# Hybrid pooling and gated-DeltaNet block on one core: the row-scale broadcast and the first pool product written as split fp32r matmuls

## The chip, the cores and the metric

One Trainium2 chip, one of its cores. The kernel is one program, launched once. The metric is the device time of that launch in microseconds. The engines are named as the profile names them: PE is TensorE (PEld its weight loads), DVE is VectorE, ACT is ScalarE, POOL is GpSimd, SP is SyncE. A "q" behind an engine's name means its queue, for instance SPq for the transfers that SP issues.

## What is computed

One decoder block on x of 2048 rows by 1024 columns, all in float32, cut here to what the change touches:

```
n    = x * rsqrt(mean(x*x, per row) + eps) * norm_w          # row scale r = rsqrt(...)
proj = n @ w_in                                               # 1024 -> 3080 columns
pool_u, pool_z, q, k, v, z, b, a = split(proj)
# pool branch: 4 groups of 128 channels, trailing windows 2, 4, 8, 16
mix  = trailing_mean(pool_u, window of the group) - pool_u
pool = (mix @ pool_w[group]) * pool_scale * silu(pool_z)
# DeltaNet branch: 4 heads of 128, causal conv of width 4 on q, k, v, chunked delta rule
h    = x + [pool ; deltanet] @ w_out
out  = rms_norm(h, final_norm_w)
```

## The kernel before

**Layout of the work.** The 2048 rows are worked in two blocks (`b` 0 and 1) of 1024 rows, each in two halves (`hf` 0 and 1) of 512. Channels lie on the 128 partitions and rows along the free axis, so that a projection tile is a 128x512 PSUM tile. Products that must be accurate are made of split operands: a float32 value is written as a high part in fp32r and a low part, the remainder, in fp32r, and three fp32r matmuls (high by high, high by low, low by high) are added in PSUM. `project` (L727) does this with eight contraction steps of three matmuls each (L733, L734, L735). Other products are single float32 matmuls, which the profile shows as two PE instructions each.

**The row scale.** The projections multiply x times norm_w; the row scale r is applied to the result. For each half, `square_x` (L531) sums the squares of the eight column tiles on ACT, DVE and POOL. `row_scale` (L543) sums them over the partitions with four one-column float32 matmuls into `pss`, computes r by an integer guess and three Newton steps on 128x4 tiles (DVE, L501 to L508), and writes four 128x128 diagonal matrices `dg`, ident times r (L557, a tile with the tag `sacc`). `broadcast` (L559) multiplies a matrix of ones by these 512 columns in float32 (`psr`, L561), which puts r of each row on all partitions, and ACT copies the result to `rb` (L563). Each evacuation of a projection tile out of PSUM multiplies by `rb` (L742, L758, L771), and so does the gate's (L574). No PSUM bank of a half's projections comes free before its `rb` is there.

**The pool branch.** In each half, `pool_mix` (L767) makes the mix of a group. For groups 1 to 3 the pool weights have been multiplied into the projection weights (`mix_weights`, L691), and `pool_out` (L794) only scales. For group 0, `pool_out` multiplies mix by `pw[:, 0]` in one float32 matmul of 512 columns (`pm`, L798), and DVE scales the result out of PSUM (L800).

**What sets the order.** Each step is entered with a slot number (`at(slot, function)`), and slots give the program order. `Planner.run` then makes the order of each engine: a list schedule over all instructions with a cost for each (L123, where a float32 matmul of 512 columns is put at 860 ns and an fp32r one at 226 ns), with latest times computed backwards, in which PE takes whole groups of matmuls and may take a group up to 24 places ahead if it can start sooner (L282 to L292), and the other engines take the most urgent ready instruction unless that would delay a more urgent one. Each engine executes the order so made, strictly in turn. `L_ROW0`, `L_RB` and the like are hand-set distances in slots. Tiles come from rings by tag: `acc` has three buffers, `sacc`, `ps_s` and `sqj` two, `tmp` and `X` one; a new tile of a tag waits until the tile that had its buffer is read for the last time.

**The opening.** `begin` (L457) loads norm_w and fills `ones`, `warm_up` (L461) runs 11 float32 matmuls on it, `load_constants` (L466) issues nine small loads on SP, `prepare_constants` (L486) makes the fp32r constants.

Of the kernel before, what the change touches and what calls it, by code (L numbers as in the profile page):

```python
# [43 lines left out]
PAIRED = 2  # L44
# [353 lines left out]
def hymba_kernel(  # L398
# [44 lines left out]
    ones = ct([P, P], F32, "ones")  # L443
    ones_r = ct([P, P], F32R, "ones_r")
    wba = ct([P, KT, 8], F32, "wba")
# [4 lines left out]
    pw = ct([P, GROUPS, P], F32, "pw")  # L450
# [5 lines left out]

    def begin():  # L457
        nc.scalar.dma_start(nw, norm_w)
        nc.vector.memset(ones, 1.0)

    def warm_up():  # L461
        ps = plan.tile(pd, [P, HALF], F32, "pd", "warm", 2, True)
        for i in range(WARM):
            nc.tensor.matmul(ps[:, 0:P], ones, ones, start=True, stop=True)

    def load_constants():  # L466
        plan.opening = len(plan.traced)
        tri = st([P, 2, P], F32, "X")
        for dst, src in (
# [6 lines left out]
            (pw, pool_w),  # L476
# [7 lines left out]
        return tri  # L484

    def prepare_constants(tri):  # L486
# [56 lines left out]
    def row_scale(env):  # L543
        ps = plan.tile(pd, [P, HALF], F32, "pd", "pss", 2, True)
        for j in range(NCH):
            nc.tensor.matmul(
                ps[:, j : j + 1], env["ss"][:, j * P : (j + 1) * P], ones[:, 0:1], start=True, stop=True
            )
# [6 lines left out]
        env["dg"] = dg = st([P, NCH, P], F32, "sacc", 2)  # L555
        for j in range(NCH):
            nc.vector.tensor_scalar(out=dg[:, j], in0=ident, scalar1=r[:, j : j + 1], scalar2=None, op0=ALU.mult)  # L557

    def broadcast(env):  # L559
        ps = plan.tile(pd, [P, HALF], F32, "pd", "psr", 2, True)  # L560
        nc.tensor.matmul(ps, ones, env["dg"].rearrange("p a b -> p (a b)"), start=True, stop=True)  # L561
        env["rb"] = rb = st([P, HALF], F32, "rb", 3)
        nc.scalar.copy(rb, ps)  # L563
# [127 lines left out]
    def mix_weights(gi, m, part):  # L691
        ks = slice(part * NCH, (part + 1) * NCH)
        ps = plan.tile(pd, [P, NCH, P], F32, "pd", "pw", 2, True)
        for j in range(NCH):
            nc.tensor.matmul(ps[:, j], m["wT"][:, part * NCH + j], pw[:, gi], start=True, stop=True)
# [71 lines left out]
    def pool_mix(u, b, gi, hf, rb):  # L767
# [24 lines left out]
        )  # L792

    def pool_out(u, b, gi, hf, res, mixed_w):  # L794
        pm = u["mix"]
        if not mixed_w:
            pm = plan.tile(pp, [P, HALF], F32, "pp", "pm", 3, True)
            nc.tensor.matmul(pm, pw[:, gi], u["mix"], start=True, stop=True)  # L798
# [299 lines left out]
    lead = 1  # L1098
    for i, gi in enumerate(range(lead, GROUPS)):
# [4 lines left out]
    tri = []  # L1104
    at(-90, begin)
    at(-89, warm_up)
    at(-45, lambda: tri.append(load_constants()))
    at(-1, lambda: prepare_constants(tri[0]))
    for b in range(NB):
# [5 lines left out]
        for gi, res in pools[:lead]:  # L1115
# [4 lines left out]
        for gi, res in pools[lead:]:  # L1120
# [39 lines left out]
        for (kind, et, idx, res), hf in order:  # L1160
            if et not in weights:
                weights[et] = {"mixed": kind == "pu" and idx >= lead}
# [383 lines left out]
```

## Time and profile before

| what | value |
|---|---|
| time, median of 3 runs | 945.32 us (944.15 to 946.16) |
| time of the profiled execution | 946.3 us |
| its span, first to last instruction | 944.6 us |
| granted TensorE clock, mean | 0.995 of full |
| PE busy | 917.4 us, 97% |
| DVE busy | 659.9 us, 70% |
| ACT busy | 467.3 us, 49% |
| POOL busy | 146.9 us, 16% |

The profile records one execution. Its span leaves out 1.7 us of the 946.3 us around the first and the last instruction. Matmuls overlap in the records: a matmul's own duration is longer than the distance to the next one's start, and that distance is what it costs in a stream. "Idle before" an instruction is time in which its engine ran nothing, and the name behind the arrow is the instruction whose end released it.

### The profile page before, as it was taken

The page shows a single profiled execution, that of the slowest core. Times are in us where ns is not written, and L with a number is a line of the kernel's source. Part 1 is how long each engine was busy: PE and PEld are TensorE (multiplying, and loading weights), DVE is VectorE, ACT ScalarE, POOL GpSimd, SP SyncE. Part 2 cuts the span into 40 slices and gives each one's busy share as a digit, 9 for nine tenths or more (in the row PEclk, how much of TensorE's full clock was granted, in tenths as well). Part 3 has the DMA queues.
Part 4 walks back from the last instruction along what each step waited for, and adds up shares of the span by engine and source line. Part 5 has one row for each costly group of instructions (what it writes and reads, how often), then busy time and mean ns, then how long its engine had stood idle before and what let it go on. Part 6 is the DMA issues. An engine that isn't in the chain of part 4 may idle for free.

```text
span 944.6 us, 15009 instructions
## 1 busy us (share of the span) xinstructions
PE 917.4 (97%) x5226; PEld 741.2 (78%) x5226; DVE 659.9 (70%) x1963; ACT 467.3 (49%) x1209; POOL 146.9 (16%) x195
## 2 busy tenths in 40 slices
PE   8999999999999999999999999999999999999995
PEld 6667888888888877768888787887887788788884
DVE  7587976867768455865886774875854578987665
ACT  7338654464464245534945544545533435444441
POOL 3206210110100012302610010011001000011110
PEclk9999999999999999999999999999999999999998
DMA  8424564344433554434345343334247487466644
GB/s 290 107 57 95 140 168 106 67 100 93 94 89 87 156 146 141 103 74 89 97 104 115 73 89 86 73 84 112 56 119 252 120 230 227 140 168 168 165 104 122
DMA packets 82268, 115.84 MB, mean 123 GB/s; under 512 B 31888, under 2 KB 49552, under 8 KB 82192
## 3 DMA queue, kind: packets, MB, share of 16 engines
q0 software_dynamic: 17280, 56.89, 27.6%
q1 hardware_dynamic: 64480, 57.46, 19.6%
q8 instruction: 41, 0.67, 0.3%
q10 hardware_dynamic: 432, 0.53, 0.2%
q14 instruction: 35, 0.29, 0.1%
HBM read 92.83 MB, written 22.02 MB: 122 GB/s over the span
## 4 chain that ended last, share of the span: by engine, by line
PE 70%; DVE 9%; issue 8%; DMA 6%; ACT 3%; POOL 1%; SPq 1%; DVEq 0%; ACTq 0%; POOLq 0%
PE ps L733 14%; PE ps L735 13%; PE ps L734 13%; PE psA L1399 2%; PE psA L1400 2%; PE psA L1401 2%; PE tp L825 2%; PE ch L1012 2%; PE ch L990 1%; DMA wl<-in_w_in_dram 1%; PE ch L1006 1%; PE ob L1000 1%; PE ob L1016 1%; PE psC L1401 1%; PE psC L1400 1%
## 5 line engine op out<-in xcount | busy, mean ns | idle before, releaser
L733 PE MATMUL ps<-nh,wh 128*128 128x512 f32 x768 | 326.1, 425 | 0.9 <-ACT nh L526 0.4
L735 PE MATMUL ps<-nh,wl 128*128 128x512 f32 x768 | 302.4, 394 | 2.4 <-DMA wl<-in_w_in_dram 2.4
L734 PE MATMUL ps<-nl,wh 128*128 128x512 f32 x768 | 301.4, 392 | 2.2 <-DVE nl L527 2.2
L735 PEld LDWEIGHTS ps<-nh,wl 128*128 128x128 f32 x768 | 144.5, 188 | 35.6 <-DMA wl<-in_w_in_dram 4.1
L734 PEld LDWEIGHTS ps<-nl,wh 128*128 128x128 f32 x768 | 145.7, 190 | 27.1 <-DVE nl L527 5.0
L733 PEld LDWEIGHTS ps<-nh,wh 128*128 128x128 f32 x768 | 145.5, 189 | 26.2 <-issue 1.6
L747 DVE SCALAR_TENSOR_TENSOR acc<-u,cw,acc 128x512 f32<-128x512 f32 x144 | 109.5, 760 | 19.0 <-ACT acc L745 16.7
L716 POOL DMA_DIRECT2D wh<-in_w_in_dram x40 | 22.3, 557 | 342.5 <-PE ps L735 330.3
L742 DVE TENSOR_TENSOR u<-ps,rb 128x512 f32<-128x512 f32 x48 | 33.1, 689 | 51.4 <-PE ps L735 51.2
L724 ACT ACTIVATE wl<-wh 128x1024 fp32r<-128x1024 f32 x40 | 42.5, 1061 | 47.9 <-DMA wh<-in_w_in_dram 34.9
L725 POOL DMA_DIRECT2D wl<-in_w_in_dram x40 | 34.8, 871 | 186.6 <-ACT wl L724 146.9
L905 DVE TENSOR_TENSOR tmp<-Ai,X 128x60 f32<-128x60 f32 (+24 forms) x248 | 53.4, 215 | 7.4 <-DMA Ai<-blocks 1.6
L911 DVE TENSOR_TENSOR X<-X,tmp 128x60 f32<-128x60 f32 (+24 forms) x248 | 53.6, 216 | 6.2
L745 ACT ACTIVATE acc<-u,cw 128x512 f32<-128x512 f32 x48 | 34.9, 727 | 45.6 <-DVE u L742 43.3
L1019 ACT ACTIVATE sqj<-v 128x128 f32<-128x128 f32 x64 | 19.7, 308 | 65.8 <-DVE v L1017 59.6
L1008 ACT ACTIVATE nv<-ch,sm 128x128 f32<-128x128 f32 x64 | 23.5, 368 | 32.1 <-PE ch L1006 32.1
L1407 POOL DMA_DIRECT2D dec<-in_x_dram x23 | 19.7, 854 | 122.8 <-ACT dec L1406 69.7
L1013 DVE SCALAR_TENSOR_TENSOR state<-state,ex,ch 128x128 f32<-128x128 f32 x64 | 22.0, 344 | 20.7 <-PE ch L1012 19.9
L832 ACT ACTIVATE sqj<-tp 128x128 f32<-128x128 f32 x128 | 33.7, 278 | 4.5 <-PE tp L825 4.3
L1002 ACT ACTIVATE o<-ob,ex 128x128 f32<-128x128 f32 x64 | 23.6, 369 | 18.8 <-PE ob L1000 17.8
L1012 PEld LDWEIGHTS ch<-nv,kdec 128*128 128x128 f32 x128 | 19.7, 189 | 13.5 <-ACT nv L1008 12.9
L1006 PEld LDWEIGHTS ch<-rho,Tt 128*128 128x128 f32 x128 | 22.3, 189 | 8.2 <-DVE rho L992 4.6
(299 smaller groups left out, 1768.6 us busy)
## 6 DMA issues: line engine op xcount, KB each, us to landing
wh<-in_w_in_dram POOLq DMA_DIRECT2D x40, 512.0 KB, 3.9
wl<-in_w_in_dram POOLq DMA_DIRECT2D x40, 512.0 KB, 5.5
y_dram<-yt SPq DMA_DIRECT2D x32, 256.0 KB, 2.9
out_dram<-dec SPq DMA_DIRECT2D x14, 512.0 KB, 3.7
dec<-in_x_dram POOLq DMA_DIRECT2D x23, 256.0 KB, 4.1
Ai<-blocks SPq DMA_DIRECT2D x32, 128.0 KB, 2.6
yr<-y_dram SPq DMA_DIRECT2D x8, 512.0 KB, 4.8
dec<-in_xT_dram SPq DMA_DIRECT2D x7, 512.0 KB, 6.6
```

The costliest lines, as they stand in the source:

```text
L724: nc.scalar.activation(w["lo"], w["hi"].bitcast(F32), AF.Copy, scale=-1.0)
L725: nc.gpsimd.dma_start(w["lo"], w_in[et], accum_op=ALU.add)
L733: nc.tensor.matmul(ps, w["hi"][:, k], nh[:, k], start=(k == 0), stop=False)
L734: nc.tensor.matmul(ps, w["hi"][:, k], nl[:, k], start=False, stop=False)
L735: nc.tensor.matmul(ps, w["lo"][:, k], nh[:, k], start=False, stop=(k == KT - 1))
L742: nc.vector.tensor_tensor(out=ub[:, HALO:], in0=ps, in1=rb, op=ALU.mult)
L745: nc.scalar.activation(acc, ub[:, HALO:], AF.Copy, scale=cw[:, ci, CONV - 1 : CONV])
L747: nc.vector.scalar_tensor_tensor(out=acc, in0=ub[:, h0 + j : h0 + j + HALF], scalar=cw[:, ci, j : j + 1], in1=acc, op0=ALU.mult, op1=ALU.add,)
L832: nc.scalar.activation(junk, tp[:, j], AF.Square, accum_out=dst[:, c : c + 1])
L905: nc.vector.tensor_tensor(out=tmp[:, 0:n, 0:w], in0=Ai[:, j, j + 1 : BS].unsqueeze(1).to_broadcast([P, n, w]), in1=X[:, 0:n, j : j + 1].to ...
L911: nc.vector.tensor_tensor(out=X[:, 0:n, j + 1 : BS], in0=X[:, 0:n, j + 1 : BS], in1=tmp[:, 0:n, 0:w], op=ALU.subtract)
L1012: nc.tensor.matmul(ch[:, 2], e["kdec"][:, c], nv, start=True, stop=True)
```

## The change

The ones matrix, the raw pool weights of group 0 and the raw gate weights move from tiles of their own to ring tiles (`sqj`, `sqj`, `tmp`), and the pool weights of group 0 are loaded by a DMA of their own and split once. `row_scale` splits r into a high and a low part and writes two sets of diagonal matrices, the high one on DVE (tag `sacc`) and the low one on ACT (tag `acc`); `broadcast` adds two fp32r matmuls. For group 0, `pool_mix` splits mix into a high part on ACT (tag `ps_s`) and a low part on DVE (tag `acc`), and `pool_out` adds three fp32r matmuls. `LEAD` is 1, as `lead` was.

```diff
-    ones = ct([P, P], F32, "ones")
+    onec = ct([P, 1], F32, "onec")
     ones_r = ct([P, P], F32R, "ones_r")
-    wba = ct([P, KT, 8], F32, "wba")
...
-    pw = ct([P, GROUPS, P], F32, "pw")
+    pw = ct([P, GROUPS - LEAD, P], F32, "pw")
+    pwr = ct([P, 2, P], F32R, "pwr")
...
     def begin():
         nc.scalar.dma_start(nw, norm_w)
+        nc.vector.memset(onec, 1.0)
+
+    def warm_up():
+        raw["ones"] = ones = st([P, P], F32, "sqj", 2)
         nc.vector.memset(ones, 1.0)
-
-    def warm_up():
...
-        tri = st([P, 2, P], F32, "X")
+        raw["tri"] = tri = st([P, 2, P], F32, "X")
+        raw["wba"] = wba = st([P, KT, 8], F32, "tmp")
+        raw["pw"] = pw0 = st([P, LEAD, P], F32, "sqj", 2)
...
-            (pw, pool_w),
+            (pw0, pool_w[:, 0:LEAD]),
+            (pw, pool_w[:, LEAD:]),
...
-    def prepare_constants(tri):
+    def prepare_constants():
+        tri, wba, pw0, ones = (raw[k] for k in ("tri", "wba", "pw", "ones"))
+        nc.scalar.copy(pwr[:, 0], pw0[:, 0])
+        nc.vector.tensor_tensor(out=pwr[:, 1], in0=pw0[:, 0], in1=pwr[:, 0], op=ALU.subtract)
...
-                ps[:, j : j + 1], env["ss"][:, j * P : (j + 1) * P], ones[:, 0:1], start=True, stop=True
+                ps[:, j : j + 1], env["ss"][:, j * P : (j + 1) * P], onec, start=True, stop=True
...
-        env["dg"] = dg = st([P, NCH, P], F32, "sacc", 2)
+        rh = st([P, NCH], F32R, "rh", 2)
+        nc.vector.tensor_copy(rh, r)
+        rl = st([P, NCH], F32, "rl", 2)
+        nc.vector.tensor_tensor(out=rl, in0=r, in1=rh, op=ALU.subtract)
+        dh = st([P, NCH, P], F32R, "sacc", 2)
+        dl = st([P, NCH, P], F32R, "acc", 3)
+        env["dg"] = (dh, dl)
         for j in range(NCH):
-            nc.vector.tensor_scalar(out=dg[:, j], in0=ident, scalar1=r[:, j : j + 1], scalar2=None, op0=ALU.mult)
+            js = slice(j, j + 1)
+            nc.vector.tensor_scalar(
+                out=dh[:, j], in0=ident, scalar1=rh.bitcast(F32)[:, js], scalar2=None, op0=ALU.mult
+            )
+            nc.scalar.activation(dl[:, j], ident, AF.Copy, scale=rl[:, js])
 
     def broadcast(env):
         ps = plan.tile(pd, [P, HALF], F32, "pd", "psr", 2, True)
-        nc.tensor.matmul(ps, ones, env["dg"].rearrange("p a b -> p (a b)"), start=True, stop=True)
+        for i, dg in enumerate(env["dg"]):
+            nc.tensor.matmul(ps, ones_r, dg.rearrange("p a b -> p (a b)"), start=(i == 0), stop=(i == 1))
...
-            nc.tensor.matmul(ps[:, j], m["wT"][:, part * NCH + j], pw[:, gi], start=True, stop=True)
+            nc.tensor.matmul(ps[:, j], m["wT"][:, part * NCH + j], pw[:, gi - LEAD], start=True, stop=True)
...
+        if gi < LEAD:
+            u["split"] = mh, ml = st([P, HALF], F32R, "ps_s", 2), st([P, HALF], F32R, "acc", 3)
+            nc.scalar.copy(mh, mix)
+            split_lo(nc.vector, ml, mix, mh)
...
-            nc.tensor.matmul(pm, pw[:, gi], u["mix"], start=True, stop=True)
+            mh, ml = u["split"]
+            nc.tensor.matmul(pm, pwr[:, 0], mh, start=True, stop=False)
+            nc.tensor.matmul(pm, pwr[:, 0], ml, start=False, stop=False)
+            nc.tensor.matmul(pm, pwr[:, 1], mh, start=False, stop=True)
```

## Rows read from the trace of the kernel before

**Rows 1.** The page's head and its first part: span; then an engine's busy time, share of the span and instructions.

```profile
span 944.6 us, 15009 instructions
...
PE 917.4 (97%) x5226; PEld 741.2 (78%) x5226; DVE 659.9 (70%) x1963; ACT 467.3 (49%) x1209; POOL 146.9 (16%) x195
```

**Rows 2.** The page's fourth part, the chain of work that ended last, as shares of the span by engine.

```profile
PE 70%; DVE 9%; issue 8%; DMA 6%; ACT 3%; POOL 1%; SPq 1%; DVEq 0%; ACTq 0%; POOLq 0%
```

**Rows 3.** The view of waits, of PE alone: engine, line, what it waited for; us in total, times, longest us.

```profile
PE ps L735 <- DMA wl<-in_w_in_dram: 2.4, 3, 1.2
```

**Rows 4.** Groups of PE instructions by line and shape: count behind the x, then busy us and mean ns of one, idle us before them.

```profile
L798 PE MATMUL pm<-acc,pw 128*128 128x512 f32 x8 | 4.3, 619 | 0.0
L561 PE MATMUL psr<-sacc,ones 128*128 128x512 f32 x8 | 4.2, 612 | 2.2 <-DVE sacc L557 2.2
```

**Rows 5.** The timeline of PE and of its weight loads (PEld) in the first projections, three fp32r matmuls of 512 columns to a contraction step.

```profile
17.09 0.39 PE L733 MATMUL ps<-nh,wh 128*128 128x512 f32 x1
17.09 0.19 PEld L734 LDWEIGHTS ps<-nl,wh 128*128 128x128 f32 x1
17.32 0.39 PE L734 MATMUL ps<-nl,wh 128*128 128x512 f32 x1
```

**Rows 6.** The timeline of PE in the second block, around the last pool product of group 0: start us, us, engine, line.

```profile
433.12 1.02 PE L798 MATMUL pm<-acc,pw 128*128 128x512 f32 x2
...
434.22 0.40 PE L734 MATMUL ps<-nl,wh 128*128 128x512 f32 x1
```

**Rows 7.** The chain of waits in the second block, in order of time: start us, us on the chain, what. Line 662 adds two fp32r matmuls of 512 columns in one bank.

```profile
442.37 0.46 PE psd L662 x2
```

**Rows 8.** The timeline of all engines around the second broadcast (first block, second half).

```profile
46.89 0.88 DVE L557 TENSOR_SCALAR sacc<-cst,rstd 128x128 f32<-128x128 f32 x4
47.12 1.06 ACT L724 ACTIVATE wl<-wh 128x1024 fp32r<-128x1024 f32 x1 [6.90 <-DMA wh<-in_w_in_dram]
...
47.91 1.10 PE L561 MATMUL psr<-sacc,ones 128*128 128x512 f32 x2 [1.03 <-DVE sacc L557]
...
49.08 0.39 PE L570 MATMUL psba<-nl,whl 128*8 128x512 f32 x1
```

**Rows 9.** The timeline of DVE ahead of the third broadcast (second block, first half).

```profile
404.23 0.16 DVE L508 SCALAR_TENSOR_TENSOR rstd<-nr_a,rstd 128x4 f32<-128x4 f32 x1
...
406.43 0.17 DVE L508 SCALAR_TENSOR_TENSOR rstd<-nr_a,rstd 128x4 f32<-128x4 f32 x1
406.50 0.75 DVE L800 SCALAR_TENSOR_TENSOR yt<-acc,psc,szp 128x512 f32<-128x512 f32 x1
407.17 0.89 DVE L557 TENSOR_SCALAR sacc<-cst,rstd 128x128 f32<-128x128 f32 x4
```

**Rows 10.** The timeline of PE around the third broadcast.

```profile
406.59 0.39 PE L735 MATMUL ps<-nh,wl 128*128 128x512 f32 x1
408.20 1.10 PE L561 MATMUL psr<-sacc,ones 128*128 128x512 f32 x2 [1.22 <-DVE sacc L557]
...
409.36 0.40 PE L734 MATMUL ps<-nl,wh 128*128 128x512 f32 x1
```

**Rows 11.** The timeline of ACT ahead of the third broadcast.

```profile
405.36 1.05 ACT L724 ACTIVATE wl<-wh 128x1024 fp32r<-128x1024 f32 x1
409.33 0.59 ACT L563 COPY rb<-psr 128x512 f32<-128x512 f32 x1 [2.92 <-PE psr L561]
```

**Rows 12.** The timeline of PE around the first broadcast (first block, first half).

```profile
28.83 1.03 PE L561 MATMUL psr<-sacc,ones 128*128 128x512 f32 x2
...
29.93 0.39 PE L734 MATMUL ps<-nl,wh 128*128 128x512 f32 x1
```

**Rows 13.** The timeline of all engines ahead of the fourth broadcast (second block, second half).

```profile
414.79 0.88 DVE L557 TENSOR_SCALAR sacc<-cst,rstd 128x128 f32<-128x128 f32 x4
...
419.06 1.02 PE L561 MATMUL psr<-sacc,ones 128*128 128x512 f32 x2
```

**Rows 14.** The timeline of all engines in the first block, around the second pool product of group 0.

```profile
51.60 0.69 DVE L790 SCALAR_TENSOR_TENSOR acc<-ps_s,u 128x512 f32<-128x512 f32 x1
...
54.51 0.67 DVE L574 TENSOR_TENSOR ba<-psba,rb 16x512 f32<-16x512 f32 x1
...
55.24 0.42 PE L581 MATMUL tp<-cst,ba 16*128 16x16 f32 x4 [0.47 <-DVE ba L574]
...
55.59 1.12 PE L798 MATMUL pm<-acc,pw 128*128 128x512 f32 x2
```

**Rows 15.** The instructions of single lines: engine, operation, tiles, count; ns at least, median, at most; first and last start; forms.

```profile
L623 DVE CAST gh<-g x2: 181/182/182, 62.0 to 433.5; 128x32 fp32r<-128x32 f32 x2
...
L624 DVE TENSOR_TENSOR gl<-g,gh x2: 191/192/192, 62.2 to 433.8; 128x32 fp32r<-128x32 f32 x2
...
L721 ACT CAST wh<-qT x4: 602/611/620, 5.6 to 15.4; 128x512 fp32r<-128x512 f32 x4
...
L511 DVE TENSOR_TENSOR ps_s<-pw,yt x6: 683/689/693, 109.9 to 152.4; 128x512 fp32r<-128x512 f32 x6
```

**Rows 16.** The timeline of ACT at the end of a head in the second block: eight activations of 128x128 with a scale per partition.

```profile
689.77 2.45 ACT L1031 ACTIVATE v<-v,f 128x128 f32<-128x128 f32 x8 [0.23 <-DVE f L508]
```

**Rows 17.** The timeline of all engines in the opening: an issue of SP and the first reader of what it loads.

```profile
18.18 0.33 SPq L480 DMA_DIRECT2D nega<-in_a_log_dram  x1
...
24.53 0.19 ACT L492 ACTIVATE nega<-nega 128x4 f32<-128x4 f32 x1
```

More of the change, by code (lines that the diff above doesn't have):

```diff
@@ L43 @@
 L_ROW0, L_SQ1, L_SQB, L_X, L_GR0, L_GR, L_GCOL = (16.0, 18.0), 13.5, -40, 44, 21.5, 5.5, 2.75
-PAIRED = 2
+PAIRED, LEAD = 2, 1
 X_TAGS = (
@@ L455, in hymba_kernel @@
     state = ct([P, HEADS, P], F32, "state")
+    raw = {}
     def begin():
         nc.scalar.dma_start(nw, norm_w)
+        nc.vector.memset(onec, 1.0)
+    def warm_up():
+        raw["ones"] = ones = st([P, P], F32, "sqj", 2)
         nc.vector.memset(ones, 1.0)
-    def warm_up():
         ps = plan.tile(pd, [P, HALF], F32, "pd", "warm", 2, True)
@@ L483, in load_constants @@
         nc.gpsimd.memset(state, 0.0)
-        return tri
-    def prepare_constants(tri):
+    def prepare_constants():
+        tri, wba, pw0, ones = (raw[k] for k in ("tri", "wba", "pw", "ones"))
+        nc.scalar.copy(pwr[:, 0], pw0[:, 0])
+        nc.vector.tensor_tensor(out=pwr[:, 1], in0=pw0[:, 0], in1=pwr[:, 0], op=ALU.subtract)
         nc.scalar.copy(whl[:, :, 0:8], wba)
@@ L1097, in hymba_kernel @@
     slot = 0
-    lead = 1
-    for i, gi in enumerate(range(lead, GROUPS)):
+    for i, gi in enumerate(range(LEAD, GROUPS)):
         m = {}
@@ L1103, in hymba_kernel @@
             at(L_MIX + 20 * i + 4 * part, mix_weights, gi, m, part)
-    tri = []
     at(-90, begin)
     at(-89, warm_up)
-    at(-45, lambda: tri.append(load_constants()))
-    at(-1, lambda: prepare_constants(tri[0]))
+    at(-45, load_constants)
+    at(-1, prepare_constants)
     for b in range(NB):
@@ L1114, in hymba_kernel @@
         tiles = []
-        for gi, res in pools[:lead]:
+        for gi, res in pools[:LEAD]:
             tiles += [("pu", E_PU + gi, gi, res), ("pz", E_PZ + gi, gi, res)]
@@ L1119, in hymba_kernel @@
             tiles += [(kind, e0 + h, h, res) for kind, e0 in kinds]
-        for gi, res in pools[lead:]:
+        for gi, res in pools[LEAD:]:
             tiles += [("pu", E_PU + gi, gi, res), ("pz", E_PZ + gi, gi, res)]
@@ L1161, in hymba_kernel @@
             if et not in weights:
-                weights[et] = {"mixed": kind == "pu" and idx >= lead}
+                weights[et] = {"mixed": kind == "pu" and idx >= LEAD}
                 first = ("qT", 2) if slot < 8 * PAIRED else None
```

## The prediction

> **What bounds the kernel now.** The page comes first: PE is busy for 97% of the span [rows 1], and the chain of work that ended last runs on PE for most of its length [rows 2]. So an instruction taken from PE's stream shortens the time by its place in that stream, unless PE then waits. The view of waits says how thin the cover is: the longest kind of wait is only 2.4 us in all, for weights by DMA [rows 3], and next to it, told by the groups of PE, are 2.2 us ahead of the broadcast [rows 4]. What a matmul costs is read as a distance between starts, not from its own duration: fp32r matmuls of 512 columns follow each other by 0.23 us, while each lasts 0.39 us [rows 5].
>
> **The change part by part.** *The float32 products.* Eight PE instructions at each of two lines are four calls of two instructions [rows 4]. The pool product starts at 433.12 and the second projection matmul behind it at 434.22; less 0.23 us for the projection matmul between them, the product holds PE for 0.87 us [rows 5, 6]. The first broadcast gives the same, 29.93 less 28.83 less 0.23 [rows 12].
>
> *What replaces the broadcast.* An existing pair of fp32r matmuls of 512 columns adds 0.46 us to the chain [rows 7]. Each of four broadcasts so gives back 0.87 - 0.46 = 0.41 us of PE, 1.64 us in all, as far as PE has other work until the operands are there.
>
> *What replaces the pool product.* Three fp32r matmuls are 3 x 0.23 = 0.69 us; four times 0.18 us is 0.72 us. The new loads count too. In the trace a weight load of 0.19 us begins together with the matmul before its own and is gone by the time that its own starts, 0.23 us later [rows 5]. So loads add nothing. The Trainium skill (TensorE: Matmul & The Clock Gate, "The mechanism") says otherwise: a load overlaps matmuls in flight only where it addresses other rows of the array. The trace disagrees with it, since these loads and matmuls use all 128 rows; by that rule the change would cost time, and it stands below as a rival.
>
> *The longer row-scale chain.* Before, r is followed by four diagonal writes on DVE from 407.17 (0.89 us), a hand-over of 0.14 us and the product on PE from 408.20 until 409.13 (409.36 less 0.23): 1.96 us in all [rows 9, 10]. After, the longest branch is: cast to the high part and subtraction on 128x4. Their nearest rows are 128x32: the subtraction starts 0.2 us behind the cast and lasts 0.19 us [rows 15], so 0.39 us. Then a hand-over to ACT, 0.14 us by the one above; four scaled activations of 128x128 at 2.45 / 8 = 0.31 us, 1.22 us [rows 16]; a hand-over of 0.14 us; and the last fp32r matmul, 0.23 us. That is 2.12 us. The high diagonals (DVE, 0.39 + 0.89 us) and the first fp32r matmul lie beside it. So where PE waits for this chain, the change gives no 0.41 us; it costs 0.16 us, say 0.2. Lower bound: if the low branch took nothing beyond the high one, the chain would be the cast, the high diagonals, a hand-over and the pair, 0.2 + 0.89 + 0.14 + 0.46 = 1.69 us, a gain of 0.27 us. The upper bound stands with the second rival. I take the 0.2 us, since each of its terms has a row of its own kind.
>
> *Where PE waits for it.* At the second broadcast PE stood idle for 1.03 us until the diagonals came [rows 8], at the third for 1.22 us [rows 10]. These two go by the chain: 2 x 0.2 = 0.4 us lost. At the first PE runs on without a gap [rows 12], and at the fourth the diagonals are done at 415.7 and PE comes at 419.06 [rows 13]; these two go by PE's stream: 2 x 0.41 = 0.82 us won. At the first, the later low diagonals are covered by projection groups that the planner can take ahead; without that cover it costs the same 0.2 us instead of winning 0.41.
>
> *Splitting mix.* The high part is an ACT cast of 0.61 us and the low part a DVE subtraction of 0.69 us [rows 15], ahead of each pool product. I take nothing for them. The tightest place has mix ready at 52.29 and the product at 55.59 [rows 14], 3.3 us for 1.3 us of work. Behind the subtraction on DVE stands the gate's evacuation (54.51), for which PE's transpose at 55.24 waited 0.47 us [rows 14]; if the planner puts the subtraction ahead of it, up to 0.69 us is lost once.
>
> *Constants.* The load of group 0's weights is one more issue on SP, 0.33 us, and pushes the later small loads back; the last of these is issued at 18.18 and first read at 24.53 [rows 17]. The split of these weights (a 128x128 cast and a subtraction, each under the 0.31 us of an ACT instruction of that shape [rows 16]) is due before the first pool product. Both at nothing; were the split put into the opening's DVE chain, some 0.3 us. The moved tiles are read for the last time in the opening, long before their rings are needed again. The low diagonals and the low part of mix now take turns in `acc`, one of three buffers each, so a square or a conv accumulator may wait for a broadcast or a pool product; I price this within the range.
>
> *Sum.* 0.82 + 0.72 - 0.4 = 1.1 us off. The profiled execution took 946.3 us, 1.0 us over the median of the runs; the same 1.1 us off the median, 945.3, gives **944.2 us**. That is 0.12%; 0.2% (1.9 us) is about the least that a measurement of this kernel can tell from no change.
>
> **The rivals.** *First, faster: the planner covers the longer chain.* All orders are made anew, and PE may take projection groups from up to 24 places ahead. If it fills the waits at the second and third broadcast, all four give 0.41 us: 1.64 + 0.72 = 2.36 us, 942.9 us. For it: two of four broadcasts are covered now. Against it: at the other two PE found nothing to run. If the idle 1.03 us and 1.22 us shrink as well, it goes further, by my estimate to 941.3 us.
>
> *Second, slower: the new links wait their turn.* DVE and ACT work strictly in order, and the change adds two links on DVE and one on ACT to the chain at its most urgent place. At the third broadcast the steps of r already stand between long instructions: three links took 406.43 - 404.23 = 2.20 us, 0.73 us each [rows 9] where a link alone takes 0.2 us. Two more of these cost 2 x 0.53 = 1.06 us, and a weight cast of 1.05 us as seen on ACT just before [rows 11], put ahead of the low diagonals, 1.05 us more. At the second broadcast that cast starts at 47.12 [rows 8], just before the low diagonals are due at 46.89 + 0.39 + 0.14 = 47.42; it would hold them until 48.18, 0.76 us. With the 0.69 us at the gate that makes 3.56 us, less the 1.1 us: 2.5 us slower, 947.8 us. It decides the sign from 1.1 us of such delay, and passes 0.2% from 3.0 us. For it: that very cast was on ACT at that time. Against it: the planner knows these instructions and lets no less urgent one delay them by more than its slack, and ACT stood idle for 2.92 us at the third [rows 11].
>
> *Third, the price of loads.* If each fp32r matmul had to wait for its own load, a pair would cost 2 x 0.42 = 0.84 us and three 1.26 us: the pool products lose 4 x 0.39 = 1.56 us, the two covered broadcasts win 0.06 us, and the two waiting chains, longer by 0.19 us each, lose 0.78 us. That is 2.3 us slower, 947.6 us. It is the rule of the page named above; every row of fp32r matmuls speaks against it.
>
> *Fourth, the new order.* Some 5200 matmuls are ordered afresh, and waits far from the change, such as the 2.4 us for weights [rows 3], may come or go. It has no sign.
>
> **How the numbers follow.** The forecast, 0.3 to 1.9 us off (943.4 to 945.0 us on its own), has 0.47; the first rival 0.34; the second 0.14; the third 0.01; the fourth 0.04, shared alike by gain, loss and neither. Faster by over 0.2% is the first rival and a part of the fourth, 0.35; slower is the second, the third and a part of the fourth, 0.17; the rest, 0.48, is within 0.2%. The range, 941.3 to 947.0 us, takes in the first rival to its end and the delays of the second up to 2.8 us, and leaves out the rest.
>
> **What would show it.** In the profile after: two instructions of fp32r at the broadcast and three at the pool product, PE's busy time down; distances of 0.46 us and 0.69 us where there were 0.87 us; the idle time ahead of the second and third broadcast or between its two matmuls longer, by about 0.6 us each, released by ACT's low diagonals; no wait of the pool product for the low part of mix. The prediction is wrong if those waits vanish or shrink (first rival), if low diagonals follow a weight cast or a gap of over 1 us behind r (second), or if the difference lies at places that the change doesn't touch (fourth).

## The result, and the profile after

The change made the kernel slower: 947.61 us in the median of 14 runs (945.39 to 949.86) against 945.23 us (943.90 to 947.19, 14 runs) for the kernel before in the same sets. The ratio is 1.0026, with an interval of 1.0017 to 1.0035. The profiled execution of the changed kernel is the longest of its 14, 949.86 us, 2.25 us above its median, and that of before (946.3 us) 1.1 us above its own; the stages are compared with that in mind. First its head, against [rows 1]:

```profile
span 948.1 us, 15048 instructions
...
PE 917.6 (97%) x5230; PEld 740.6 (78%) x5230; DVE 660.4 (70%) x1977; ACT 475.8 (50%) x1230; POOL 146.5 (15%) x195
```

PE's busy time did not fall, 917.6 us after 917.4 us. Yet the products are what they were meant to be: two fp32r matmuls at the broadcast, three at the pool product. The instructions of the broadcast's line, high and low part (ns at least, median, at most; first and last start), and the first pool product in the timeline:

```profile
L581 PE MATMUL psr<-sacc,ones_r x4: 392/432/472, 29.4 to 427.2; 128*128 128x512 f32 x4
...
L581 PE MATMUL psr<-acc,ones_r x4: 394/449/504, 29.6 to 427.5; 128*128 128x512 f32 x4
```

```profile
38.21 0.39 PE L823 MATMUL pm<-ps_s,pwr 128*128 128x512 f32 x1
...
38.44 0.40 PE L824 MATMUL pm<-acc,pwr 128*128 128x512 f32 x1
...
38.67 0.39 PE L825 MATMUL pm<-ps_s,pwr 128*128 128x512 f32 x1
```

Three starts 0.23 us apart where [rows 6] had 0.87 us for one product. So the saving is there, matmul by matmul, and something takes more than that back. The timeline of all engines between the two broadcasts of the first block (after) shows what changed first:

```profile
28.11 1.28 ACT L576 ACTIVATE acc<-cst,rl 128x128 fp32r<-128x128 f32 x4 [3.48 <-issue]
...
35.91 1.06 ACT L744 ACTIVATE wl<-wh 128x1024 fp32r<-128x1024 f32 x1 [1.01 <-DMA wh<-in_w_in_dram]
...
36.41 0.67 DVE L520 TENSOR_TENSOR acc<-acc,ps_s 128x512 fp32r<-128x512 f32 x1
36.88 1.13 ACT L548 ACTIVATE acc<-kdec 128x512 f32<-128x512 f32 x2
...
38.88 1.98 ACT L548 ACTIVATE acc<-kT 128x512 f32<-128x512 f32 x3 [0.86 <-PE pm L824]
...
43.83 0.69 DVE L550 TENSOR_TENSOR sacc<-sacc,acc 128x512 f32<-128x512 f32 x1 [1.47 <-POOL sacc L550]
44.58 1.05 PE L555 MATMUL pss<-onec,sacc 128*128 128x1 f32 x8 [0.74 <-DVE sacc L550]
```

In the kernel before, the same squares of kdec and the last sum of squares stand here:

```profile
32.38 1.14 ACT L539 ACTIVATE acc<-kdec 128x512 f32<-128x512 f32 x2
...
41.74 0.69 DVE L541 TENSOR_TENSOR sacc<-sacc,acc 128x512 f32<-128x512 f32 x1 [1.46 <-POOL sacc L541]
```

The squares of kdec start 4.5 us later. They are `acc` tiles, and so are now the low diagonals (28.11) and the low part of mix (36.41). In the order made for ACT the squares now stand behind a weight cast that waits for its DMA (35.91), where before they stood ahead of it, and those of kT wait 0.86 us until PE has read the low part of mix (pm L824). Some of that is made up, and the sum of squares is ready 2.1 us late (43.83 against 41.74). PE waits 0.74 us for it, and then for the second broadcast:

```profile
48.32 1.28 ACT L576 ACTIVATE acc<-cst,rl 128x128 fp32r<-128x128 f32 x4 [1.15 <-DVE rl L567]
48.34 0.67 DVE L573 TENSOR_SCALAR sacc<-cst,rh 128x128 fp32r<-128x128 f32 x3
49.16 0.47 PE L581 MATMUL psr<-sacc,ones_r 128*128 128x512 f32 x1 [2.05 <-DVE sacc L573]
...
50.35 0.63 PE L590 MATMUL psba<-nl,whl 128*8 128x512 f32 x1
50.78 0.63 PE L589 MATMUL psba<-nh,whl 128*16 128x512 f32 x1
```

That is 2.79 us of waiting where [rows 8] had 1.03 us. The two psba matmuls show the second loss: 0.43 us apart, where they were 0.23 us apart. The view of windows (stretch in us, its length, then busy us of each engine, the granted TensorE clock third from the end) says why; the kernel before has 1.00 in all four stretches:

```profile
48.00:50.00 2.00, 0.82 (x3) 0.40 (x4) 1.90 (x9) 1.28 (x4) 0.33 (x1) 1.00 0.44 41
50.00:52.00 2.00, 2.00 (x6) 0.65 (x5) 1.21 (x3) 0.59 (x1) 0.00 (x0) 0.51 0.98 193
52.00:54.00 2.00, 2.00 (x7) 0.74 (x6) 1.61 (x5) 1.16 (x3) 0.00 (x0) 0.63 0.16 29
54.00:56.00 2.00, 2.00 (x11) 1.19 (x9) 1.88 (x3) 0.72 (x2) 0.00 (x0) 1.00 0.00 0
```

Behind the wait the clock is at its lower level, 1.2 GHz, for most of 50 to 54 us: eight matmuls at 0.43 in place of 0.23 us, 1.6 us of PE's busy time. (The 917.4 us of before hold a loss of the same kind, at 580 us; the run of the order alone, below, shows its size.)

How far the change lies behind as a whole is read where both kernels have run the same number of projection matmuls. These are the 133rd and the 445th, each of the kernel before and then of the change:

```profile
57.24 0.39 PE L733 MATMUL ps<-nh,wh 128*128 128x512 f32 x1
...
59.22 0.40 PE L753 MATMUL ps<-nh,wh 128*128 128x512 f32 x1
...
162.22 0.47 PE L733 MATMUL ps<-nh,wh 128*128 128x512 f32 x1
...
166.76 0.48 PE L753 MATMUL ps<-nh,wh 128*128 128x512 f32 x1
```

So it is 1.98 us behind after the second broadcast and 4.54 us behind at 162 us, where nothing was changed. The 2.6 us in between are mostly waits: two of the small products `y` for `td` (0.47 and 0.52 us, shown with the experiments), and this one, 1.50 us where the kernel before has 0.43 us (first line):

```profile
161.75 0.49 PE L1012 MATMUL ch<-nv,kdec 128*128 128x128 f32 x2 [0.43 <-ACT nv L1008]
...
164.93 1.06 ACT L744 ACTIVATE wl<-wh 128x1024 fp32r<-128x1024 f32 x1 [2.05 <-DMA wh<-in_w_in_dram]
165.89 0.35 ACT L1035 ACTIVATE nv<-ch,sm 128x128 f32<-128x128 f32 x1
166.29 0.49 PE L1039 MATMUL ch<-nv,kdec 128*128 128x128 f32 x2 [1.50 <-ACT nv L1035]
```

Here too a weight cast that waits for its DMA stands ahead of what PE needs on ACT. At the third and fourth broadcast 1.3 us come back (4.67 us behind at 404 us, 3.37 us at 425 us).

At the third broadcast the chain on DVE and ACT looks as the second rival had it, and PE still waits less than the 1.22 us of [rows 10]:

```profile
411.06 0.16 DVE L517 SCALAR_TENSOR_TENSOR rstd<-nr_a,rstd 128x4 f32<-128x4 f32 x1
...
411.79 0.17 DVE L565 CAST rh<-rstd 128x4 fp32r<-128x4 f32 x1
...
412.52 0.17 DVE L567 TENSOR_TENSOR rl<-rstd,rh 128x4 f32<-128x4 f32 x1
...
413.62 0.47 PE L581 MATMUL psr<-sacc,ones_r 128*128 128x512 f32 x1 [0.62 <-DVE sacc L573]
```

PE runs six projection matmuls more ahead of this broadcast (1185 where the kernel before has 1179), which is the cover that the first rival spoke of.

### The profile page after: what moved, and what is told of

It is laid out like the page before. It is cut to its first block, busy times and chain, and to the rows that moved or that the text cites. A ratio compares the mean times of both kernels' runs of the same rounds, so it can differ in the third digit from the quotient of the medians.

```text
span 948.1 us, 15048 instructions
## 1 busy us (share of the span) xinstructions
PE 917.6 (97%) x5230; PEld 740.6 (78%) x5230; DVE 660.4 (70%) x1977; ACT 475.8 (50%) x1230; POOL 146.5 (15%) x195
## 4 chain that ended last, share of the span: by engine, by line
PE 68%; DVE 12%; issue 8%; DMA 8%; ACT 2%; POOL 2%; SPq 1%; DVEq 0%; POOLq 0%; ACTq 0%
PE ps L753 13%; PE ps L755 12%; PE ps L754 12%; DMA wl<-in_w_in_dram 2%; PE psA L1424 2%; PE psA L1425 2%; PE psA L1426 2%; PE tp L852 2%; DVE X L938 2%; DVE tmp L932 1%; PE ch L1039 1%; PE ch L1017 1%; DVE acc L767 1%; PE ch L1033 1%; PE kk L878 1%
## 5 line engine op out<-in xcount | busy, mean ns | idle before, releaser
L1039 PE MATMUL ch<-nv,kdec 128*128 128x128 f32 x128 | 27.6, 297 | 1.7 <-ACT nv L1035 1.5
```

What stands on the lines that cost most here:

```text
L1039: nc.tensor.matmul(ch[:, 2], e["kdec"][:, c], nv, start=True, stop=True)
```

## The experiments

Each was timed against the kernel before on the same chip; "over" and "under" are differences of the medians of one set. Line numbers in the rows are those of each kernel.

**Low parts out of the ring `acc`.**

```diff
-        dl = st([P, NCH, P], F32R, "acc", 3)
+        dl = st([P, NCH, P], F32R, "yt", 2)
...
-  mh, ml = st([P, HALF], F32R, "ps_s", 2), st([P, HALF], F32R, "acc", 3)
+  mh, ml = st([P, HALF], F32R, "ps_s", 2), st([P, HALF], F32R, "yt", 2)
```

> The changed kernel, with its two low parts (of the row scale and of mix) in the ring yt instead of acc; the arithmetic is the same. Theory A (ring): the squares of the second half of the first block share acc with the low parts, so they start 4.5 us later than before (36.88 for 32.38) and the second broadcast 1.25 us later; PE's clock then falls. It expects the squares of kdec to start before the low part of mix is written, the second broadcast to start at about 48.3 instead of 49.16, PE's wait ahead of it near 1.2 us instead of 2.05, no granted clock under 1.0 between 48 and 56 us, and a time 1 to 2.5 us under the changed kernel (about 945 to 946.5). Theory B (the links of the split alone): the wait stays at 1.8 to 2.1 us and the clock still falls, time within 0.7 us of the changed kernel. Theory C (the new order elsewhere costs it): the wait ahead of the second broadcast may shrink, but the time stays within 1 us of the changed kernel, as other waits (131 us, 166 us in the changed kernel) remain or come.

949.89 us, 1.0048 (1.0033 to 1.0062): the slowest of all. The timeline at its second broadcast:

```profile
46.05 0.47 PE L581 MATMUL psr<-sacc,ones_r 128*128 128x512 f32 x1
...
48.85 1.06 ACT L744 ACTIVATE wl<-wh 128x1024 fp32r<-128x1024 f32 x1 [9.75 <-DMA wh<-in_w_in_dram]
49.82 1.26 ACT L576 ACTIVATE yt<-cst,rl 128x128 fp32r<-128x128 f32 x4
...
51.13 0.80 PE L581 MATMUL psr<-yt,ones_r 128*128 128x512 f32 x1 [4.61 <-ACT yt L576]
```

The high half of the broadcast comes 3.1 us earlier than in the change and PE does not wait for it, so `acc` had held it: off it, ACT squares kdec from 32.44 us on, ahead of the weight cast of 35.90 us. But now the low diagonals are due before the next weight cast, stand behind it in ACT's order, and the cast waits 9.75 us for its DMA. The time expected of the ring's theory was missed because of this second mechanism, which is the second rival's weight cast, "put ahead of the low diagonals", with the DMA's delay on top.

**The broadcast's split alone**, the pool product left as before.

> The row scale and its broadcast split as in the change, the pool product of group 0 left in float32 with its raw weights. Theory A: half of the ring's load (the low diagonals hold back only the first square); squares of kdec start at 33 to 35, second broadcast at about 48.3 to 48.7; time 0 to 1 us over the kernel before. Theory B: the second broadcast waits about 2 us as in the change and the loss is here, 1.5 to 3 us over before. Theory C: any, within 3 us of before.

946.44 us, 1.0007 (0.9997 to 1.0017). Here too the cast is in the way:

```profile
47.11 1.06 ACT L739 ACTIVATE wl<-wh 128x1024 fp32r<-128x1024 f32 x1 [6.96 <-DMA wh<-in_w_in_dram]
48.07 1.26 ACT L571 ACTIVATE acc<-cst,rl 128x128 fp32r<-128x128 f32 x4
...
49.39 0.74 PE L576 MATMUL psr<-acc,ones_r 128*128 128x512 f32 x1 [0.71 <-ACT acc L571]
```

PE waited 1.30 us for the high and 0.71 us for the low diagonals, and the clock was 0.50 from 50 to 52 us. The squares of kdec started at 33.60 us.

**The pool product's split alone**, the broadcast left as before.

> The pool product of group 0 split as in the change, the broadcast left in float32. Theory A: the low part of mix sits in acc ahead of the squares of kdec, which start near 36.9 as in the change; second broadcast about 1 us later than before, time 0.5 to 2 us over before. Theory B: no link is added to the row scale, so the second broadcast starts as before (47.9, wait 1.0 us) and the time is 0.7 us under before. Theory C: any, within 3 us of before.

945.61 us, 1.0003 (0.9991 to 1.0016): no loss and no gain beyond the interval, which still holds the 0.72 us of the sum. At the second broadcast it waited 1.02 us, at clock 1.00. The squares of kdec started at 33.73 us, not at the 36.9 us that the ring's theory expected of it. So the low part of mix alone puts the squares 1.35 us later, the low diagonals alone (the run before) 1.22 us, and in both runs the sum of squares is no later than in the kernel before; only both together make the 4.5 us.

**The order alone**: the kernel before, with its planner's cost of a float32 matmul of 512 columns at 460 in place of 860 ns.

> The kernel before with one number of the planner changed: a float32 matmul of 512 columns is put at 460 ns instead of 860 ns when the order is made. The instructions are the same, only their order may differ. Theory A and theory B: within 1 us of before. Theory C (a new order by itself moves the time): more than 1.5 us off before, either way.

944.35 us, 0.9993 (0.9983 to 1.0003). It tests less than its name says: PE ran the same 5226 matmuls in the same order as in the kernel before. But it is of use as a second profile of that stream. In it the clock stayed at 1.00 from 580 to 590 us, where the profile of before fell to 0.83, and PE's busy time was 915.6 us, not 917.4.

**Low diagonals on DVE, off `acc`**: the first run's edit, and

```diff
-            nc.scalar.activation(dl[:, j], ident, AF.Copy, scale=rl[:, js])
+            nc.vector.tensor_scalar(out=dl[:, j], in0=ident, scalar1=rl[:, js], scalar2=None, op0=ALU.mult)
```

> As the run with both low parts in the ring yt, and the low diagonals written by DVE instead of ACT. Theory D (queue): in that run the low diagonals stood on ACT behind a weight cast that waited for its DMA until 48.85, with their input ready at 45.1; that made the 4.61 us of PE's wait, and the wait brought the lower clock. On DVE they are not behind it: second broadcast's high matmul at 46 to 46.5, its low one by 47.4, PE idle there 0.5 to 1.5 us in all, granted clock 1.0 from 30 to 60 us, time 943 to 945 us, 4 to 6 us under that run and at or under the kernel before. Theory B (the links themselves): PE idle over 2 us, time over 947. Theory C (new order): the wait may go, but the time stays over 947.

944.72 us, 1.0000 (0.9987 to 1.0014): 0.14 us under the kernel before, where the first run was 4.39 us over it. At the second broadcast:

```profile
46.98 0.47 PE L581 MATMUL psr<-sacc,ones_r 128*128 128x512 f32 x1 [0.56 <-DVE rl L567]
...
47.87 0.51 PE L581 MATMUL psr<-yt,ones_r 128*128 128x512 f32 x1 [0.42 <-DVE yt L576]
```

0.98 us of waiting and clock 1.00: both mechanisms removed, the time is level with the kernel before, though the split stands at all four broadcasts.

**Low diagonals on DVE, `acc` kept.**

> The changed kernel with the low diagonals written by DVE instead of ACT, both low parts in acc as in the change. Theory A+D: in the change the cast was done before the low diagonals were due, so little is won there: the second broadcast starts within 0.3 us of 49.16, its wait stays near 2 us, the clock falls, and the time is within 1 us of the changed kernel (946.5 to 948.5).

947.60 us, 1.0023 (1.0011 to 1.0036). Here ACT writes no diagonals, and the loss is that of the change all the same. The ring alone sets this kernel apart from the run before, in the same set: 2.88 us. PE waited 2.01 and 0.22 us, clock 0.55 and 0.59 in the two stretches from 50 to 54 us.

**The wait filled**: the change with ten fp32r matmuls on old operands ahead of the second broadcast, which overwrites what they leave.

```diff
+        for _ in range(fill):
+            nc.tensor.matmul(ps, ones_r, env["n"][0][:, 0], start=True, stop=True)
```

> The changed kernel with ten fp32r matmuls of 512 columns that nobody reads put ahead of the second broadcast, in its own PSUM tile; they have 2.27 us of PE and may run while PE waits. The wait for the diagonals stays; only PE's idleness goes. Theory E (the lower clock behind the wait is part of the loss): granted clock 1.0 from 48 to 56 us, matmuls of the gate rows 0.23 us apart instead of 0.43, and 1 to 1.7 us less than the changed kernel (945.9 to 946.6). If the clock does not matter: within 0.5 us of the changed kernel.

946.72 us, 1.0017 (1.0007 to 1.0027); clock 1.00 from 48 to 56 us. 0.5 us less loss than the change (1.86 us over against 2.38 us), where 1 to 1.7 us were expected, and the broadcast comes 0.3 us later (49.49 us). In the right direction, too small to settle the clock's share by itself.

**The split undone at the second broadcast.**

> The changed kernel with the split undone at the second broadcast alone (float32 diagonals and one float32 matmul there). Theories A, D and E: the loss sits at the second broadcast; undoing the split there takes the links away but leaves the squares late (low part of mix in acc): second broadcast 0.3 to 0.8 us earlier than in the change, time 1 to 2.5 us under it (945 to 946.6). Theory C: within 1 us of the changed kernel.

946.22 us, 1.0014 (1.0002 to 1.0025), 1.36 us over; it waited 0.75 us for the sums of squares, which the ring still holds, and 1.73 us for the diagonals, at clock 1.00.

**A late broadcast and nothing else**, and **the same, filled** with the ten matmuls of the fill above: the kernel before, the diagonals of its second broadcast written three times.

```diff
-        for j in range(NCH):
+        for j in list(range(NCH)) * reps:
```

> The kernel before, with the four diagonals of the second broadcast written three times instead of once (8 more DVE writes of 0.22 us, 1.78 us in all), and nothing else: the wait of PE there should be 1.0 + 1.8 = 2.8 us. If a late broadcast costs its wait alone, the time is 1.8 us over the kernel before. If the granted clock falls behind such a wait, as in the changed kernel, the stretch from 50 to 54 us shows 0.5 to 0.8 and some 1.6 us more are lost: 3.4 us over the kernel before.

> The run of the late diagonals again, with ten fp32r matmuls of 512 columns on old operands ahead of the second broadcast (the broadcast overwrites what they add up). If the loss behind the wait is the clock's, the clock stays at 1.00 there and the time is 1.8 us over the kernel before, 1.6 us less than the run without them; if the clock has no part, both runs take the same.

947.56 us, 1.0031 (1.0019 to 1.0043), 2.87 us over; filled, 945.26 us, 1.0009 (1.0000 to 1.0017), 0.57 us over, where 1.8 us were expected. The windows of the first, then of the filled one:

```profile
50.00:52.00 2.00, 2.00 (x6) 0.51 (x4) 0.75 (x3) 0.59 (x1) 0.00 (x0) 0.56 0.99 139
52.00:54.00 2.00, 2.00 (x7) 0.72 (x6) 2.00 (x5) 1.10 (x2) 0.00 (x0) 0.59 0.64 127
```

```profile
50.00:52.00 2.00, 2.00 (x10) 0.82 (x9) 1.17 (x3) 0.59 (x1) 0.00 (x0) 1.00 0.85 147
52.00:54.00 2.00, 2.00 (x11) 0.94 (x9) 2.00 (x5) 1.25 (x2) 0.00 (x0) 1.00 0.49 98
```

PE's wait was 2.65 us unfilled (broadcast at 49.55) and 0.17 us filled (49.09). So matmuls that compute nothing make the kernel 2.3 us shorter, and no part of the change is in these two kernels. The streams, compared as above, say where this comes from. At the first projection matmul behind the gate's rows the filled kernel is 2.02 us ahead (53.75 against 55.77 us): 0.46 us is the earlier broadcast, 1.56 us is the clock's, about the 1.6 us read from the distances. Then 0.5 us is lost again at the gate, for whose evacuation the filled kernel waits 0.48 us and the unfilled one not at all, and 1.0 us is won at 162 us, where the unfilled kernel waits 0.74 us for `nv` and the filled one not. So the 2.3 us as a whole are not a measure of the clock. The gate's wait also explains why the late broadcast costs less than the 3.4 us expected: 1.62 us of longer wait and 1.6 us of clock, less the 0.47 us that the kernel before waits at the gate [rows 14], and its stream is 2.67 us behind at 57 us.

**Second broadcast undone, off `acc`.**

> The changed kernel with the split undone at the second broadcast and with all low parts (low diagonals of the others, low part of mix) in the ring yt in place of acc. Against the run with the second broadcast undone alone (946.22 us, 1.36 us over the kernel before in its set) only the ring differs. If the acc ring holds back the squares, the wait ahead of the second broadcast falls from 1.73 us behind 0.75 us to about 1.0 us, and the time is some 1 us less: within 0.5 us of the kernel before. If the ring does not matter, it stays 1.4 us over it.

946.96 us, 1.0023 (1.0013 to 1.0033): missed. Its `pss` started at 41.75 us, 2.85 us earlier than in the run before that still had the ring, and PE did not wait for the broadcast at all (46.09). So the ring's effect on the second broadcast is shown. But the lead was lost behind the next link:

```profile
48.54 1.06 ACT L751 ACTIVATE wl<-wh 128x1024 fp32r<-128x1024 f32 x1 [9.27 <-DMA wh<-in_w_in_dram]
49.51 0.57 ACT L590 COPY rb<-psr 128x512 f32<-128x512 f32 x1
50.10 0.69 DVE L798 TENSOR_TENSOR u<-ps,rb 128x512 f32<-128x512 f32 x1 [2.72 <-ACT rb L590]
...
55.44 0.42 PE L608 MATMUL tp<-cst,ba 16*128 16x16 f32 x4 [2.55 <-DVE ba L601]
```

The broadcast was done at 47.11 us, but ACT copies it to `rb` only behind the weight cast, at 49.51 us, no earlier than in the kernel before (49.04 us). DVE stood idle for 2.72 us until then, and the gate's evacuation came at 54.71 us (54.51 us before). So PE waited 2.55 us there and was level with the kernel before at 57 us. The 2.27 us over it arose later, as in the change: at 162 us it was 3.2 us behind, with waits of 0.71 us for kT, 0.93 us of y for `td` and 1.11 us for `nv`.

**The split where it is covered**: first and fourth broadcast and the pool product, low diagonals on DVE, low parts in `yt`.

> The version that the runs point to: the split only where PE does not wait for the broadcast (first and fourth), the second and third in fp32 as before, the pool product split, low diagonals on DVE, all low parts in yt. By the sum 0.82 + 0.72 = 1.5 us under the kernel before, about 943.6 us, if nothing else moves. If the order elsewhere decides (as the run of the pool product alone suggests, which showed its 0.9 us in the profile and not in the time), it is equal to the kernel before within 0.5 us.

944.68 us, 1.0001 (0.9992 to 1.0010). PE's busy time was 915.7 us. That is 1.7 us less than in the profile of the kernel before, but not less than the 915.6 us of the run of the order alone, whose clock did not fall at 580 us. So it shows none of the 1.54 us of the sum. The kernel was ahead of the kernel before by 1.9 us at the gate product `qp` (90.20 against 92.09 us, of which 0.7 us are three projection matmuls fewer ahead of it), and level with it at a product of pool weights at 150 us (150.06 and 150.07), behind the same number of projection matmuls. In between lie 1.1 us of waits of a transpose for kT and of the small products y for td. With the pool product's split PE takes y 27 projection matmuls earlier than in the kernel before, and waits there; in the change:

```profile
131.27 0.24 PE L972 MATMUL y<-td,At 32*32 32x32 f32 x2 [0.47 <-DVE td L964]
...
132.03 0.69 PE L972 MATMUL y<-td,At 32*32 32x32 f32 x30 [0.52 <-DVE td L964]
```

**y put back**, in the change, in the covered version, in the pool product alone, and in the kernel before as the control. One number of the planner puts y where the kernel before has it:

```diff
-            return 550, 2300 + 12.5 * min(kb, 256) + 1.7 * max(0, kb - 256)
+            late = 1000 if outs[0].bass_ap.tensor.name.startswith("Tt") else 0
+            return 550, late + 2300 + 12.5 * min(kb, 256) + 1.7 * max(0, kb - 256)
```

> The changed kernel with one number of the planner altered: a transfer into the tile Tt is taken to land 1 us later, which puts the small products y of the first head 27 projection matmuls later in PE's order, where the kernel before has them. If the order is the second part of the loss, the waits of y for td (0.47 and 0.52 us) vanish, the lag of the pool weights' product at 150 us falls from 3.5 to about 2.6 us, and the time is some 0.9 us less than the changed kernel's, about 1.5 us over the kernel before. If the waits of y cost nothing, it stays 2.4 us over it.

> The version that splits only the covered broadcasts and the pool product, with the same planner number. Without the waits of y and kT (1.1 us) its lead of 1.2 us at the first gate product should still be there at 150 us: about 1.0 us under the kernel before. If the lead is given back at another place, or the waits cost nothing, it is equal to it.

> The pool product alone, with the same planner number. Without the waits of y (0.6 us): 0.3 to 0.8 us under the kernel before, where the run without it was 0.1 over. If the order has no part, 0.1 over again.

> The control: the kernel before with the same planner number alone. There y stands at the later place already, so the time should be that of the kernel before within 0.3 us. A gain or loss here is one of the order elsewhere and has to be taken off the three other runs.

All four became faster, by 1.9 to 2.5 us against the kernel before, the control by 2.35 us:

| kernel with the number | us | ratio to the kernel before | against the control |
|---|---|---|---|
| the change | 944.50 | 0.9996 (0.9987 to 1.0005) | +2.23 us |
| split where covered | 942.49 | 0.9970 (0.9957 to 0.9982) | +0.22 us |
| pool product alone | 942.85 | 0.9979 (0.9968 to 0.9991) | +0.58 us |
| the kernel before | 942.27 | 0.9967 (0.9954 to 0.9979) | - |

The waits of y for `td` went, but the control gained 2.35 us without ever having had them, so at least that much is one of the order elsewhere. PE's idle time from 500 to 600 us is 0.93 us in the control and 2.88 us in the kernel before; 1.55 us of it are two waits that the control has not, and behind them the profile of before had its clock at 0.83:

```profile
577.63 0.69 PE L957 MATMUL xx<-Tt,td 32*32 32x32 f32 x32 [1.08 <-ACT td L949]
...
578.80 0.66 PE L825 MATMUL tp<-cst,kT 128*128 128x128 f32 x4 [0.47 <-ACT v L898]
```

Taken off, the change costs 2.23 us with the number and 2.38 us without. Each has about 0.9 us of noise either way, so my reason, that y carries 0.9 us of the loss, is not confirmed, and not excluded. Three versions beat the kernel before clear of noise, and the fastest of them, though by less than the noise, holds none of the change.

Without the waits of y, the covered version lost its lead all the same. It was 0.85 us ahead of the control at 119 us and 0.37 us at 160 us, and then 0.75 us behind, at a wait that the control has not; the control's cast stood at 159.09 us:

```profile
159.84 1.06 ACT L752 ACTIVATE wl<-wh 128x1024 fp32r<-128x1024 f32 x1 [1.43 <-DMA wh<-in_w_in_dram]
...
161.21 0.49 PE L1047 MATMUL ch<-nv,kdec 128*128 128x128 f32 x2 [0.89 <-ACT nv L1043]
```

The load of these weights was issued 0.37 us earlier than in the control (154.38 against 154.75 us), and yet the cast could start only 0.75 us later. Why that load takes longer is not shown.

## Why the prediction was wrong

**The prices of the new matmuls were right, the sum was not.** The pair (0.46 us), the three of the pool product (0.69 us) and the loads that add nothing came out as put. The third rival is out: the fp32r matmuls of the pool product started 0.23 us apart, each with a load of 0.19 us. The Trainium skill (TensorE: Matmul & The Clock Gate, "The mechanism") lists that a load overlaps matmuls in flight only where it addresses other rows; this trace, too, disagrees. It is in keeping with a sentence ahead of that list, which also allows the overlap where the load goes to the background weight buffer.

**The step that failed first is the ring: "so a square or a conv accumulator may wait for a broadcast or a pool product; I price this within the range", that is, at nothing in the sum, as was the splitting of mix ("I take nothing for them").** I looked for what waits for the low part by data. What waited was a square, for a buffer. With both low parts in `acc`, the squares got a later place in ACT's order and, behind it, 0.86 us of waiting for the pool product. The ring alone is worth 2.88 us (low diagonals on DVE, with and without `acc`), the waits and the clock behind them together. The wait at the second broadcast was forecast at 1.03 + 0.2 us and became 0.74 + 2.05 us. Taking the ring away moved `pss` 2.85 us forward (the second broadcast undone, with and without `acc`), and the high half of the broadcast 3.1 us (first run).

**The second rival's mechanism is real, but at the second broadcast another one came before it.** In the change the weight cast ended at 47.16 us, before the low diagonals were due, so ACT's queue cost nothing there: with the diagonals on DVE and `acc` kept, the loss is the same (2.74 and 2.38 us). It takes over when the ring is out of the way: 4.61 us in the first run, 0.71 us with the broadcast alone. The rival's price, 0.76 us, left out that the cast itself waits for a DMA, and that other work than the low diagonals stands behind such casts: `rb` at 49.51 us with the second broadcast undone off `acc`, `nv` at 161 to 166 us. At the third broadcast its 0.73 us for each of the two new links came out exactly. PE's wait fell all the same, to 0.62 us, where 1.22 + 0.2 us were forecast, since PE found six projection matmuls to run ahead: there the first rival had it right.

**What no step held is the clock.** I priced a wait at its length. At the second broadcast the loss behind it is about as large: 1.6 us by the distances, 1.56 us between the two late broadcasts without any of the change. The change's executions say the same. In ten of the 14 the mean granted clock was 0.994 or 0.995, and they took 948.0 us in the mean; in four it was 0.996 or 0.997, and they took 946.0 us. A mean does not say where the clock fell, but it makes it likely that the loss does not come in every execution.

**What the second broadcast cost, and what it did not.** 1.8 us of longer waits and 1.6 us of clock are 3.4 us. Less the first broadcast's 0.41 us, 0.36 us at two pool products, the 0.47 us of waiting at the gate that is gone and 0.13 us of an earlier start, that is 2.0 us, as the streams show at 57 us (1.98 us). That the medians differ by a like amount, 2.38 us, is luck: the change then loses 2.6 us more up to 162 us, by the order at y and by waits for ACT, wins back 1.3 us at the third and fourth broadcast, and the rest goes either way. From 577 us on the two profiles no longer compare, since before's clock fell there. The loss of 2.6 us lies where nothing was changed, which is the sign of the fourth rival.

**And the forecast's gain does not arrive.** By the sum, the covered version should have won 1.54 us; it won nothing that the runs can tell from noise, in either order (0.01 us under the kernel before, 0.22 us over the control). An instruction taken from PE's stream "shortens the time by its place in that stream, unless PE then waits" was the sentence, and PE does wait: at the gate for its evacuation, at y, at kT, at `nv`. At the gate (second broadcast undone, off `acc`) and at `nv` the work of ACT that PE needs stands behind a weight cast, and the cast waits for its weights, so there a PE that is earlier waits longer. That this holds for all of the lost gain is not shown. The order is worth as much as the change: one cost in the planner moved the time by 2.35 us, and the fourth rival, at a chance of 0.04, was far too low.

## What to carry to other kernels

When a change gives a new tile to an old ring, list who takes a buffer of that ring next and how urgent it is; a wait for a buffer does not show among the data that the new instructions need. Look on each engine that works in order for instructions that wait for a DMA: what stands behind one is no earlier for any time saved elsewhere. Price a wait of TensorE as its length and, if the rows behind it show a lower granted clock, the slower matmuls as well. And where a planner makes the order, time the kernel before with a nudged cost first, and see that the nudge did move PE's order: it shows how far order alone moves the time, here by as much as the change, in the other direction. Last, when the terms of an explanation add up to the measured difference, compare the two streams place by place before believing it.

## What the runs showed of the hardware that was not expected

Behind a wait the granted clock fell from 1.00 to its half, 1.2 GHz, for some 3 us (in the first run some 7 us), in six of the kernels (waits of 2.0 to 4.6 us in all at the second broadcast), and matmuls of 512 columns followed each other by 0.43 in place of 0.23 us. The length of the wait alone does not decide it. A wait of 2.55 us left the clock at 1.00 where PE had run without a gap from 44 to 52 us before it (second broadcast undone, off `acc`), and so did 0.75 and 1.73 us with work between them; a wait of 2.65 us behind the one-column matmuls of `pss` and 2.9 us of busy time in four lowered it. Ten matmuls on old operands kept it up. Nor does the stream alone decide it: with the same matmuls in the same order, the clock fell at 580 us in the profile of the kernel before (waits of 1.08 and 0.47 us) and stayed at 1.00 in that of the order alone (0.80 and 0.47 us). What exactly separates these cases stays open.
